# A two-layer decoder trunk: first vectors loaded from ScalarE's queue, and three early steps traced ahead of the state-space parameters

## The chip, the core and the metric

The kernel is one program on one NeuronCore of a Trainium2 chip. The core has five instruction streams that concern us: TensorE (PE in the profile, with its weight loads as PEld), VectorE (DVE), ScalarE (ACT), GpSimd (POOL) and SyncE (SP). Each stream runs its instructions in order and waits on semaphores for the others. Transfers between HBM and on-chip memory are issued by SP, ACT or POOL as one instruction each and are then carried out by the 16 DMA engines. The metric is device time in microseconds (us); lower is better.

## What is computed

The reference is two layers of a causal decoder over 512 tokens of width 1024, in float32. Only the start of layer 0 matters here:

```python
hn = rms_norm(x, norm_mix_pre[0])        # norm factor per token, gain g0 per column
z = hn @ ev_w_in                         # 1024 -> 512 q, 512 k, 512 v, 512 u
q, k, v = ...                            # rotary, then dilated attention
a_bar = exp(A * dt); b_bar = (a_bar - 1) / A * B     # S5 state-space parameters
h = scan(a_bar, einsum(b_bar, u)); y = Re(C h) + D u # S5 layer on u
x = x + rms_norm([att, glu(gelu(y))] @ ev_w_out, norm_mix_post[0])
```

Behind it come a SwiGLU feed-forward block, a second layer with a gated recurrence, and a second feed-forward block.

## The kernel before

**Matrix products.** Every product of float32 operands is split: an operand is rounded to a short-mantissa float32 (`hi`, an ACT copy at L240 for weights) and the remainder is kept (`lo`, a DVE subtraction at L241). Three matmuls, hi·hi, hi·lo and lo·hi, make one float32 product (L170 is the line of all of them). A weight chunk of two 128-row blocks is loaded by SP (L216, 256 KB for each block), split, used, and its places are given back; 22 places of 128x512 go round.

**The start of layer 0.** The program is traced in this order. `s5_first` (L308 to L316) issues six small loads from ACT's queue: the step size `s5dt`, four loads of the state-space rows `s5rows`, and a piece of the constants `cst`. `load_vecs(0, ...)` (L298) issues four loads of 8 KB from POOL's queue: the gains g0, p0, g1, p1, one row of 128 values for each partition. SP then loads x (`xtok`, eight pieces of 256 KB, L294) alternating with the u weights (`wraw_u`, eight of 256 KB), and after that the C matrix of the state-space layer and the rest. A second set of vectors goes through POOL. `turn_vecs` (L360) transposes g0 on PE so that it lies along partitions (`cols`).

`even_layer` (L1151) then works on halves h of the tokens and pairs of columns f. PE transposes x into a bank (`xps`), ACT scales it by g0 and rounds it (`xh`, L541), DVE takes the remainder (`xl`, L542), and PE accumulates u, without the norm factor, in four PSUM banks (`ub`, banks 0 to 3). The norm factor is a scalar per token and is multiplied in when u is evacuated.

After this loop `s5_params` (L910) is traced: some 80 small operations on tiles of 128x32 to 128x288, most on DVE, in long chains of dependent steps. It makes the tables' inputs `a1`, `a2`, `m1`, `m2` and the phases `ka`, `kb`. Then the norm factor (L1183 to L1196): eight squares of x with a sum on ACT (`xsq`, L1189), a power on POOL, a broadcast by PE into bank 6 (`bc_m`), and an ACT copy to on-chip memory (`bcs_m`, L405). Then u is evacuated: four DVE multiplications (`up`, L1200) of the `ub` banks by the factor, each followed by a store to a scratch buffer in HBM (`ud`, L1203), which the state-space pieces read back reordered (`s5u`).

**What follows.** `even_body` (L1212) computes q, k and v (`qkv_gemm`), each 8 blocks of weights times four token tiles t, in four banks. The banks of q are 4, 0, 1, 2, so that token tile 0 uses a free bank and tiles 1 to 3 use banks that `ub` held. Eight pieces of the state-space layer (`s5_piece`) are traced between the matmuls of q, k and v by a clock that the program counts by hand. A piece begins with a table `em` from `m1`, `m2` (L1027 to L1029) that PE transposes (`s5eps`).

**Order.** The program is traced as a list. The context is opened with `schedule_with_timeline_sim=True`, so a scheduler makes each stream's order from that list at build time: work that is ready may go ahead of work that was traced earlier, and among ready work the earlier traced goes first. From k on (`pe_order`) PE keeps the program's order.

Of the kernel before, what the change touches and what calls it, by code (L numbers as in the profile page):

```python
# [19 lines left out]
P = 128  # L20
# [74 lines left out]
def hybrid_trunk(  # L95
# [8 lines left out]
    nc = tc.nc  # L104
    dve, act, pool = nc.vector, nc.scalar, nc.gpsimd
# [4 lines left out]
    def dump(name, ap):  # L110
        if dbg is not None and name in dbg:
            nc.sync.dma_start(dbg[name], ap)
# [8 lines left out]
    def bank(name, use="main"):  # L121
        q = sets[use]
        q.append(q.pop(0))
        return psum.tile([P, 512], F32, tag=f"bank{q[-1]}", name=name)

    def side(name):
        return bank(name, "side")
# [128 lines left out]
    def wchunk(src, nk, n, nm, **kw):  # L256
        return Chunk(Raw(nk, n, nm, src), nm, **kw)
# [5 lines left out]
    def wrows(w, k0, nk, c0, nm, **kw):  # L263

        return wchunk(w[k0 * P:(k0 + nk) * P, c0:c0 + 512].rearrange("(k p) n -> p k n", p=P), nk, 512, nm, **kw)
# [20 lines left out]
    tabp = tab_cm.__enter__()  # L286
# [3 lines left out]
    vecs = [fp.tile([SP, P], F32, name=f"vec{i}") for i in range(2)]  # L290
# [4 lines left out]

    vcol = {}

    def load_vecs(i, lst):  # L298
        row = 0
        for nm, ap in lst:  # L300
            f = ap.flatten_outer_dims() if len(ap.shape) > 2 else ap
            n = int(np.prod(ap.shape)) // P
            pool.dma_start(vecs[i][row:row + n, :], f.rearrange("a (b c) -> (a b) c", c=P))
            vcol[nm] = i * SP + row
            row += n
        assert row == SP

    def s5_first():  # L308

        rows = fp.tile([SG, 4, SP], F32, name="s5rows")  # L310
        dt = fp.tile([P, SG], F32, name="s5dt0")
        nc.scalar.dma_start(dt, s5_log_dt.partition_broadcast(P))
        for i in range(2):
            nc.scalar.dma_start(rows[:, i, :], s5_a_re[0])
            nc.scalar.dma_start(rows[:, 2 + i, :], s5_a_im[0])
        nc.scalar.dma_start(cst[:, C_JR:], consts[:, C_JR:])  # L316
        s5_raw.update(rows=rows, dt=dt)
# [8 lines left out]
        s5_raw.update(drow=drow, cc=cc)  # L326

    s5_raw = {}
    s5_first()
    load_vecs(0, (("g0", norm_mix_pre), ("p0", norm_mix_post), ("g1", norm_ffn_pre), ("p1", norm_ffn_post)))  # L330
    uw = []
    for h in range(2):
        load_x(0, h)
# [76 lines left out]
    def xg_tiles(nm):  # L410
        return ([sb.tile([P, S], F32R, tag="xh", bufs=NF, name=f"xh_{nm}{f}") for f in range(NF)],
                [sb.tile([P, S], F32R, tag="xl", bufs=NF, name=f"xl_{nm}{f}") for f in range(NF)])
# [127 lines left out]
    def x_split(src, h, l, g):  # L540
        act.activation(h, src, AF.Copy, scale=g)  # L541
        return dve.scalar_tensor_tensor(l, src, g, h.bitcast(F32), op0=ALU.mult, op1=ALU.subtract)  # L542
# [608 lines left out]
    def even_layer():  # L1151
        w = ev_w_in[0]
        xh, xl = xg_tiles("m0")

        ub = [bank(f"ub{i}") for i in range(4)]
        x_first = []
        s5_turn_a()
        for h in range(2):
            for f0 in range(0, NF, 2):
                b = side(f"xps{h}{f0}")  # L1160
                for i in range(2):
                    for t in range(2):
                        o = i * HT + t * P
                        pe.transpose(b[:, o:o + P], xtok[2 * h + t][:, (f0 + i) * P:(f0 + i + 1) * P], ident)
                for i in range(2):
                    src = b[:, i * HT:(i + 1) * HT]
                    split = x_split(src, xh[f0 + i][:, HS[h]], xl[f0 + i][:, HS[h]], col("g0", f0 + i))
                    act.activation(xT[f0 + i][:, HS[h]], src, AF.Copy)
                if f0 == XSQ:
                    x_first.append(split.ins)  # L1170
                w2 = uw[f0 // 2]
                for k in (f0, f0 + 1):
                    for i in range(4):
                        mm3(ub[i][:, HS[h]], [a[:, i * P:(i + 1) * P] for a in w2(k % 2)], xh[k][:, HS[h]],
                            xl[k][:, HS[h]], k == 0, k == NF - 1)
                if h == 1:
                    w2.free()
            if h == 0:
                T = s5_turn(tabp)
                turn_vecs(0, NF)  # L1180
                turn_vecs(1)
        s5_params(tabp, T)
        ssum = sb.tile([P, NT], F32, name="ssum0")  # L1183
        sx = sb.tile([P, NT], F32, name="sx0")
        for t in range(NT):
            for h, s in enumerate((ssum, sx)):
                j = sb.tile([P, S], F32, tag="sq", bufs=2, name=f"xsq{t}{h}")
                with tc.issue_after(x_first[t // 2]):
                    act.activation(j, xtok[t][:, h * 512:(h + 1) * 512], AF.Square, accum_out=s[:, t:t + 1])  # L1189
        dve.tensor_tensor(ssum, ssum, sx, op=ALU.add)  # L1190
        r1 = rstd_of(ssum, NT, "m0")
        rq = sb.tile([P, NT], F32, name="rq")
        dve.tensor_scalar(rq, r1, -0.125, None, op0=ALU.mult)
        r = sb.tile([P, NT], F32, name="r0")
        dve.tensor_copy(r, r1)
        rb = bcast_sb(r, "m0")  # L1196
        uds = []
        for q in range(4):
            up = sb.tile([P, TC, NK], F32, tag="gt" if q < 2 else "ut", bufs=2, name=f"up{q}")
            dve.tensor_tensor(up.rearrange("p i k -> p k i")[:, :, ::-1], ub[q].rearrange("p (k i) -> p k i", i=TC),  # L1200
                              rb.rearrange("p (k i) -> p k i", i=TC), op=ALU.mult)
            ud = dr.tile([P, S], F32, name=f"ud{q}")
            nc.sync.dma_start(ud, up.rearrange("p i k -> p (i k)"))  # L1203
            uds.append(ud)
            dump(f"u{q}", up.rearrange("p i k -> p (i k)"))
        first_cm.__exit__(None, None, None)
        with tc.tile_pool(name="even", bufs=1) as lp:
            got = even_body(w, xh, xl, r, rq, uds, T, lp)
        tab_cm.__exit__(None, None, None)
        return got  # L1210

    def even_body(w, xh, xl, r, rq, uds, T, lp):  # L1212
        share(qkv=(4, 0, 1, 2, 3), s5z=(5,), s5w=(6,), s5y=(7,), turn=(2,))

        posf = sb.tile([P, HT], F32, tag="sqh", bufs=2, name="posf")[0:NT, 0:P]
# [1 line left out]
        b = bank("posps", "s5w")  # L1217
# [26 lines left out]
        def qkv_gemm(s, at_k=lambda k: None):  # L1244
            banks = [bank(f"qkv{s}{t}", "qkv") for t in range(NT)]
            for k0 in range(0, NF, 2):
                w2 = wrows(w, k0, 2, s * 512, f"qkv{s}{k0}")
                for kk in range(2):
                    k = k0 + kk
                    hi, lo = w2(kk)  # L1250
                    for t in range(NT):
                        tt = slice(t * P, t * P + P)
                        pe.matmul(banks[t], lhsT=xh[k][:, tt], rhs=hi, start=(k == 0), stop=False)
                        pe.matmul(banks[t], lhsT=xh[k][:, tt], rhs=lo, start=False, stop=False)
                        pe.matmul(banks[t], lhsT=xl[k][:, tt], rhs=hi, start=False, stop=(k == NF - 1))
                        tick()
                    at_k(k)
                w2.free()
            ts = []
            for t in range(NT):  # L1260
                of = lp.tile([P, S], F32, tag="av", bufs=4, name=f"v{t}") if s == 2 else spare(t, f"qk{s}{t}")
                o = of.rearrange("p (h d) -> p h d", d=HD)
                act.activation(of, banks[t], AF.Copy, scale=(rq if s == 0 else r)[:, t:t + 1])
                ts.append(o)
                if s < 2:

                    cb = rcs[:, t].unsqueeze(1).to_broadcast([P, HEADS, 2, RH])
                    sbb = rsn[:, t].unsqueeze(1).to_broadcast([P, HEADS, 2, RH])
                    tv = o[:, :, 0:2 * RH].rearrange("p h (a f) -> p h a f", a=2)
                    tm = lp.tile([P, HEADS, 2, RH], F32, tag="rp0", bufs=2, name=f"rp{s}{t}")  # L1270
                    dve.tensor_tensor(tm, tv[:, :, ::-1], sbb, op=ALU.mult)
                    dve.tensor_tensor(tv, tv, cb, op=ALU.mult)
                    dve.tensor_tensor(tv, tv, tm, op=ALU.add)
            return ts
# [344 lines left out]
    xh, xl, first, nsum = even_layer()  # L1619
    for f in range(NF):  # L1620
        dump(f"x1_{f}", xT[f])
    xh, xl, first, nsum = ffn(0, xh, xl, first, nsum)
# [4 lines left out]
    xh, xl, first, nsum = odd_layer(xh, xl, first, nsum)  # L1627
# [34 lines left out]
```

## Time and profile before

| what | value |
|---|---|
| time, three runs | 1175.7, 1176.76, 1180.08 us; median 1176.76 |
| the profiled execution | 1172.18 us, of which the profile's span is 1170.2 us |
| granted TensorE clock, mean | 0.995 of full |
| busy, share of the span | PE 97%, PEld 86%, DVE 75%, ACT 54%, POOL 5% |
| moved | 113.45 MB, 97 GB/s on average |

The span runs from the first to the last instruction; the 2 us around it are not in the profile. A row of the timeline gives the start, the duration, the engine, the line of the program, the operation, what it writes and reads, and in brackets how long the engine sat idle before it and what ended that. `x3` behind a row means that three like instructions are merged. ACTq and SPq are the queues of transfers on those streams: their rows are issues, not the movement of data.

### The profile page before, as it was taken

The numbers are of one execution on the slowest core, as the hardware profiler recorded it, in microseconds if no ns is written. First come the engines' busy times: TensorE is split into PE (matmuls) and PEld (weight loads), VectorE is DVE, ScalarE is ACT, GpSimd is POOL, SyncE is SP. The second block draws the span as 40 slices with busy tenths as digits, with TensorE's granted clock in tenths as the row PEclk, the third lists the DMA queues.
The fourth block names the chain that finished last, engine by engine and source line by source line (L and its number), as shares of the span: only waits on it lengthen the run. The fifth ranks groups of instructions, "written<-read, shape, count | busy, mean of one in ns | idle before, by whom it ended". The sixth has DMA issues, their size and how long they took to land.

```text
span 1170.2 us, 20253 instructions
## 1 busy us (share of the span) xinstructions
PE 1129.9 (97%) x7550; PEld 1010.3 (86%) x7550; DVE 878.1 (75%) x1841; ACT 629.2 (54%) x1290; POOL 60.5 (5%) x101
## 2 busy tenths in 40 slices
PE   6899999999999999999999999999999999999997
PEld 6777766789899999988889987889999999988886
DVE  7978875567999899983445896966999899994224
ACT  7556567446754545662243469744955455582221
POOL 2000010004000000000002200004000000000001
PEclk9899999999999999999999999999999999999999
DMA  8254420431343323332340333340253343234221
GB/s 214 97 147 123 104 73 1 141 95 28 110 119 97 91 85 106 94 121 92 114 121 1 91 91 90 121 132 1 73 144 95 91 118 95 85 123 123 93 63 72
DMA packets 165273, 113.45 MB, mean 97 GB/s; under 512 B 26820, under 2 KB 141752, under 8 KB 165176
## 3 DMA queue, kind: packets, MB, share of 16 engines
q1 hardware_dynamic: 161848, 109.94, 32.2%
q10 hardware_dynamic: 3040, 2.17, 0.7%
q8 instruction: 59, 0.97, 0.4%
q14 instruction: 38, 0.31, 0.1%
q0 software_dynamic: 288, 0.07, 0.0%
HBM read 103.75 MB, written 4.19 MB: 92 GB/s over the span
## 4 chain that ended last, share of the span: by engine, by line
PE 78%; ACT 8%; DMA 6%; DVE 5%; issue 2%; POOL 1%; SPq 0%; ACTq 0%; DVEq 0%; POOLq 0%
PE fo L170 10%; PE op_fd L170 10%; PE qkv L170 5%; PE f00b L170 5%; PE f02b L170 5%; PE f01b L170 4%; PE f11b L170 4%; PE op_mo L170 4%; PE f12b L170 4%; PE f10b L170 4%; PE gg L170 3%; PE f03b L170 2%; PE f13b L170 2%; PE xbb L170 2%; PE fd0b L170 2%
## 5 line engine op out<-in xcount | busy, mean ns | idle before, releaser
L241 DVE TENSOR_TENSOR wlo_fo<-wraw_fo,whi_fo 128x512 fp32r<-128x512 f32 x44 | 30.2, 691 | 63.6 <-PE fo L170 55.4
L170 PE MATMUL op_fd<-hi_f,whi_fd 128*128 128x512 f32 (+1 forms) x200 | 73.6, 368 | 0.0
L170 PE MATMUL op_fd<-lo_f,whi_fd 128*128 128x512 f32 (+1 forms) x200 | 73.3, 366 | 0.0
L170 PE MATMUL op_fd<-hi_f,wlo_fd 128*128 128x512 f32 (+1 forms) x200 | 72.9, 368 | 0.0
L170 PE MATMUL fo<-wlo_fo,hi_f 128*128 128x512 f32 x176 | 69.6, 395 | 0.0
L170 PE MATMUL fo<-whi_fo,lo_f 128*128 128x512 f32 x176 | 69.2, 394 | 0.0
L170 PE MATMUL fo<-whi_fo,hi_f 128*128 128x512 f32 x176 | 68.9, 396 | 0.0
L240 ACT ACTIVATE whi_fo<-wraw_fo 128x512 fp32r<-128x512 f32 x44 | 27.6, 631 | 70.2 <-DMA wraw_fo<-in_ffn_w_down_dram 43.8
L241 DVE TENSOR_TENSOR wlo_fd<-wraw_fd,whi_fd 128x512 fp32r<-128x512 f32 x44 | 30.0, 690 | 46.5 <-ACT whi_fd L240 40.4
L240 ACT ACTIVATE whi_fd<-wraw_fd 128x512 fp32r<-128x512 f32 x44 | 27.4, 629 | 55.0 <-DMA wraw_fd<-in_ffn_w_down_dram 34.2
L170 PEld LDWEIGHTS op_fd<-lo_f,whi_fd 128*128 128x128 f32 x200 | 37.7, 189 | 6.9
L170 PE MATMUL qkv<-whi_qkv,xh_m 128*128 128x512 f32 x96 | 42.1, 440 | 1.5 <-DVE up L1200 1.3
L170 PEld LDWEIGHTS op_fd<-hi_f,wlo_fd 128*128 128x128 f32 x200 | 37.7, 188 | 6.7
L170 PEld LDWEIGHTS op_fd<-hi_f,whi_fd 128*128 128x128 f32 x200 | 37.7, 188 | 6.5
L170 PE MATMUL qkv<-wlo_qkv,xh_m 128*128 128x512 f32 x96 | 39.2, 408 | 2.6 <-DVE wlo_qkv L241 2.6
L170 PEld LDWEIGHTS fo<-whi_fo,lo_f 128*128 128x128 f32 x176 | 33.1, 188 | 7.8
L170 PEld LDWEIGHTS fo<-whi_fo,hi_f 128*128 128x128 f32 x176 | 33.1, 188 | 7.7
L170 PEld LDWEIGHTS fo<-wlo_fo,hi_f 128*128 128x128 f32 x176 | 33.1, 188 | 7.5
L170 PE MATMUL qkv<-whi_qkv,xl_m 128*128 128x512 f32 x96 | 39.0, 407 | 0.0
L638 DVE TENSOR_TENSOR wraw_s_f<-wraw_f,wraw_f 128x512 f32<-128x512 f32 x40 | 27.3, 683 | 10.6 <-DMA wraw_f<-in_ffn_w_up_dram 7.5
L241 DVE TENSOR_TENSOR wlo_mo<-wraw_mo,whi_mo 128x512 fp32r<-128x512 f32 x32 | 21.4, 685 | 15.3 <-ACT whi_mo L240 15.1
L639 DVE TENSOR_TENSOR wraw_t_f<-wraw_s_f,wraw_f 128x512 f32<-128x512 f32 x40 | 27.2, 681 | 5.6 <-DMA wraw_f<-in_ffn_w_gate_dram 5.6
(1975 smaller groups left out, 4289.2 us busy)
## 6 DMA issues: line engine op xcount, KB each, us to landing
wraw_f<-in_ffn_w_gate_dram SPq DMA_DIRECT2D x88, 256.0 KB, 3.2
wraw_f<-in_ffn_w_up_dram SPq DMA_DIRECT2D x88, 256.0 KB, 3.4
wraw_fd<-in_ffn_w_down_dram SPq DMA_DIRECT2D x44, 256.0 KB, 2.7
wraw_fo<-in_ffn_w_down_dram SPq DMA_DIRECT2D x44, 256.0 KB, 2.9
wraw_qkv<-in_ev_w_in_dram SPq DMA_DIRECT2D x24, 256.0 KB, 3.5
wraw_mo<-in_ev_w_out_dram SPq DMA_DIRECT2D x16, 256.0 KB, 5.2
wraw_xb<-in_od_w_in_dram SPq DMA_DIRECT2D x16, 256.0 KB, 2.9
wraw_gg<-in_od_w_in_dram SPq DMA_DIRECT2D x16, 256.0 KB, 2.9
```

What stands on the lines that cost most here:

```text
L170: self.pin(nc.tensor.matmul(o, lhsT=lhsT, rhs=rhs, start=start, stop=stop, **kw))
L240: act.activation(hi, src, AF.Copy)
L241: eng.tensor_tensor(lo, src, hi.bitcast(F32), op=ALU.subtract)
L638: dve.tensor_tensor(s1, a21, a22, op=ALU.add)
L639: dve.tensor_tensor(s2, s1, a11, op=ALU.subtract)
```

## The change

Three things move; no arithmetic changes.

1. The four loads of g0, p0, g1, p1 are issued by ACT instead of POOL, and ahead of the six small loads that ACT issues already.
2. The weights of the first two chunks of q (k0 = 0 and 2) are traced directly after the loop over u, ahead of the norm factor, and handed to `qkv_gemm`.
3. `s5_params` is traced after the norm factor and the evacuation of u, no longer ahead of them.

```diff
-    def load_vecs(i, lst):
+    def load_vecs(i, lst, q=pool):
...
-            pool.dma_start(vecs[i][row:row + n, :], f.rearrange("a (b c) -> (a b) c", c=P))
+            q.dma_start(vecs[i][row:row + n, :], f.rearrange("a (b c) -> (a b) c", c=P))
...
     s5_raw = {}
+    load_vecs(0, (("g0", norm_mix_pre), ("p0", norm_mix_post), ("g1", norm_ffn_pre), ("p1", norm_ffn_post)),
+              nc.scalar)
     s5_first()
-    load_vecs(0, (("g0", norm_mix_pre), ("p0", norm_mix_post), ("g1", norm_ffn_pre), ("p1", norm_ffn_post)))
...
-        s5_params(tabp, T)
+        qw = {k0: wrows(w, k0, 2, 0, f"qkv0{k0}") for k0 in (0, 2)}
         ssum = sb.tile([P, NT], F32, name="ssum0")
...
             dump(f"u{q}", up.rearrange("p i k -> p (i k)"))
+        s5_params(tabp, T)
         first_cm.__exit__(None, None, None)
...
-                w2 = wrows(w, k0, 2, s * 512, f"qkv{s}{k0}")
+                w2 = (qw.pop(k0, None) if s == 0 else None) or wrows(w, k0, 2, s * 512, f"qkv{s}{k0}")
```

More of the change, by code (lines that the diff above doesn't have):

```diff
@@ L1205, in even_layer, with even_body @@
             dump(f"u{q}", up.rearrange("p i k -> p (i k)"))
+        s5_params(tabp, T)
         first_cm.__exit__(None, None, None)
         with tc.tile_pool(name="even", bufs=1) as lp:
-            got = even_body(w, xh, xl, r, rq, uds, T, lp)
+            got = even_body(w, xh, xl, r, rq, uds, T, lp, qw)
         tab_cm.__exit__(None, None, None)
         return got
-    def even_body(w, xh, xl, r, rq, uds, T, lp):
+    def even_body(w, xh, xl, r, rq, uds, T, lp, qw):
         share(qkv=(4, 0, 1, 2, 3), s5z=(5,), s5w=(6,), s5y=(7,), turn=(2,))
```

## Prediction

> **What bounds the kernel now.** I read the page first, then the waits of PE, then the timeline of the first 60 us, since everything that moves lies there. The page says PE: busy nearly all of the span, and most of the chain that ended last.
>
> ```profile
> PE 1129.9 (97%) x7550; PEld 1010.3 (86%) x7550; DVE 878.1 (75%) x1841; ACT 629.2 (54%) x1290; POOL 60.5 (5%) x101
> ...
> PE 78%; ACT 8%; DMA 6%; DVE 5%; issue 2%; POOL 1%; SPq 0%; ACTq 0%; DVEq 0%; POOLq 0%
> ```
>
> So 40 us of 1170 are not PE at work. The waits of PE in the first 150 us show those that the change could touch: the first vector, then a pair near 50 us.
>
> ```profile
> PE vps L181 <- DMA vec<-in_norm_mix_pre_dram: 5.3, 1, 5.3
> PE qkv L170 <- DVE wlo_qkv L241: 2.6, 1, 2.6
> ...
> PE qkv L170 <- DVE up L1200: 1.3, 1, 1.3
> ```
>
> The pair costs more than its waits. The busy time by stretch (stretch, length, then PE, PEld, DVE, ACT and POOL with their counts, granted clock, DMA share, GB/s) shows 25 us in which PE is nearly full, then 5.1 us with PE at 1.3, then 5.8 us at a granted clock of 0.50:
>
> ```profile
> 20.00:45.00 25.00, 24.17 (x187) 22.86 (x188) 22.82 (x80) 17.91 (x47) 1.49 (x2) 1.00 0.42 86
> ...
> 48.00:53.10 5.10, 1.31 (x5) 0.62 (x4) 5.10 (x11) 2.62 (x7) 0.10 (x1) 0.91 0.01 2
> 53.10:58.90 5.80, 5.78 (x14) 4.52 (x15) 5.80 (x11) 0.00 (x0) 0.00 (x0) 0.50 0.72 231
> ```
>
> DVE is full in both. The evacuation of u is what PE waits for there: q's token tiles 1 to 3 need the banks that `ub` holds. Its factor is ready when ACT's `bcs_m` ends at 48.07, yet DVE does other work first:
>
> ```profile
> 46.95 0.63 ACT L240 ACTIVATE whi_qkv<-wraw_qkv 128x512 fp32r<-128x512 f32 x1 [1.40 <-DMA wraw_qkv<-in_ev_w_in_dram]
> ...
> 47.49 0.58 ACT L405 ACTIVATE bcs_m<-bc_m 128x512 f32<-128x512 f32 x1
> ```
>
> ```profile
> 48.55 0.68 DVE L1027 TENSOR_TENSOR s5em<-s5b,s5m 128x512 f32<-128x512 f32 x1
> ...
> 51.37 0.75 DVE L1044 TENSOR_TENSOR s5gm<-s5cT,s5a 128x576 f32<-128x576 f32 x1
> 52.05 1.02 DVE L1200 TENSOR_TENSOR up<-ub,bcs_m 128x512 f32<-128x512 f32 x1
> ...
> 52.92 2.86 DVE L1200 TENSOR_TENSOR up<-ub,bcs_m 128x512 f32<-128x512 f32 x3
> ...
> 55.68 0.68 DVE L1029 TENSOR_TENSOR s5em<-s5em,s5tn 128x512 f32<-128x512 f32 x1
> ```
>
> What stands ahead of `up` is not `s5_params`, which the change moves; its last copy on ACT is over at 45.6:
>
> ```profile
> 45.13 0.42 ACT L1008 ACTIVATE s5m<-s5mi 64x256 f32<-64x256 f32 x1
> ```
>
> It is the tables, L1027 and L1044, traced *behind* `up` already. They went first because the scheduler held them ready sooner. So tracing `s5_params` later does not by itself bring `up` forward; it does so only if the tables, which need the results of `s5_params`, become ready later than `up`.
>
> **The change part by part.** *The four loads on ACT* come first in time. Here are ACT's first instructions, then SP's:
>
> ```profile
> 0.73 0.41 ACTq L312 DMA_DIRECT2D s5dt<-in_s_log_dt_dram  x1
> 1.18 0.44 ACTq L314 DMA_DIRECT2D s5rows<-in_s_a_re_dram  x1
> 1.65 0.44 ACTq L315 DMA_DIRECT2D s5rows<-in_s_a_im_dram  x1
> 2.12 0.44 ACTq L314 DMA_DIRECT2D s5rows<-in_s_a_re_dram  x1
> 3.76 0.32 ACTq L315 DMA_DIRECT2D s5rows<-in_s_a_im_dram  x1
> 4.85 0.35 ACTq L316 DMA_DIRECT2D cst<-in_consts_dram  x1
> 5.23 1.28 ACT L240 ACT_TABLE_LOAD   x1 [5.23 <-DMA s5rows<-in_s_a_re_dram]
> ```
>
> ```profile
> 0.73 0.39 SPq L284 DMA_DIRECT2D cst<-in_consts_dram  x1
> 1.18 0.89 SPq L294 DMA_DIRECT2D xtok<-in_x_dram  x2
> 2.11 0.43 SPq L216 DMA_DIRECT2D wraw_u<-in_ev_w_in_dram  x1
> ```
>
> Each issue takes 0.44 us, and then there are gaps: the fifth issue of ACT comes at 3.76, the sixth at 4.85. SP's queue shows what such a gap is. A weight load there waits for a load that has nothing to do with it:
>
> ```profile
> SPq L216 <- DMA s5dt<-in_s_log_dt_dram: 1.4, 1, 1.4
> ```
>
> Taking both queues in order of issue, s5dt, cst, x, s5rows, x, s5rows, u, s5rows fill eight places, and the ninth transfer waits for the first to land, the tenth for the second. I read it as eight completion slots that SP and ACT use in turn; POOL's loads, which went out every 0.5 us without a gap, are not among them. The change puts four more loads into this rotation, at its head. The times from issue to landing in the first 30 us (last number, median):
>
> ```profile
> xtok<-in_x_dram SPq DMA_DIRECT2D x8, 256.0 KB, 5.4
> ...
> s5rows<-in_s_a_im_dram ACTq DMA_DIRECT2D x2, 8.0 KB, 3.7
> ...
> s5dt<-in_s_log_dt_dram ACTq DMA_DIRECT2D x1, 16.0 KB, 3.2
> vec<-in_norm_mix_pre_dram POOLq DMA_DIRECT2D x1, 8.0 KB, 4.0
> ```
>
> If both queues go on issuing in turn, ACT's ten loads are g0, p0, g1, p1, s5dt, four s5rows, cst. The last has the slot of the first s5rows, which has the slot of p0. p0 goes out at 1.18 and lands 3.7 later at 4.88; s5rows then lands at 8.58; cst is issued, 0.35, and ACT is free at 8.93 where it was at 5.20: 3.73 later. Behind it on ACT stand the table load, the split of the first u weights and the first xh, for which PE waits. Of the delay, the idle time that ACT has there now is absorbed:
>
> ```profile
> 7.89 0.63 ACT L240 ACTIVATE whi_u<-wraw_u 128x512 fp32r<-128x512 f32 x1 [0.61 <-DMA wraw_u<-in_ev_w_in_dram]
> 8.42 0.46 ACT L541 ACTIVATE xh_m<-xps,cols 128x256 fp32r<-128x256 f32 x1
> ...
> 9.66 0.63 ACT L240 ACTIVATE whi_u<-wraw_u 128x512 fp32r<-128x512 f32 x1 [0.17 <-DMA wraw_u<-in_ev_w_in_dram]
> ```
>
> ```profile
> 8.93 1.23 PE L170 MATMUL ub<-xh_m,whi_u 128*128 128x256 f32 x4 [1.09 <-ACT xh_m L541]
> ```
>
> That is 3.73 - 0.61 - 0.17 = 2.95 us. From there to 45 us PE is full (24.17 of 25), so nothing takes it back; later x and u loads slip by 1 to 3 us by the same rotation, no more than their users. The fourth s5rows, which PE's next transposes need, takes the slot of s5dt: 3.76 + 3.2 = 7.0, landing at 10.7, before the xh that PE waits for anyhow (8.42 + 2.95 + 0.46 = 11.8). The gain on the other side is nothing: g0 comes perhaps 0.3 us sooner (3.7 against 4.0), but what PE does after `vps` needs x, and then xh from ACT. Bounds: +0.98 if no slot ever binds (four issues of 0.44 less 0.78), +5 or more if the loads land slowly. I take 2.95.
>
> The Trainium skill, "DMA: Bandwidth & Descriptors", section "Issuing engines are not separate DMA queues", says that issuing from more engines saves only the sequencer's time of issue, usually small beside the transfer. By that rule alone the move would cost ACT its issues and no more, which is the lower bound; the wait of a weight load for s5dt in this trace speaks for the higher.
>
> *The q weights and the norm factor, 0.* The first chunk is split already while `s5_params` runs, and PE can use it for token tile 0 alone until `up` has run. The factor `r` is there at 25.4, and its broadcast runs at 44.00, when the u loop leaves PE and bank 6 to it:
>
> ```profile
> 24.50 0.67 DVE L241 TENSOR_TENSOR wlo_qkv<-wraw_qkv,whi_qkv 128x512 fp32r<-128x512 f32 x1
> ...
> 25.27 0.15 DVE L1195 COPY r<-rsy_m 128x4 f32<-128x4 f32 x1
> ...
> 44.00 0.38 PE L170 MATMUL bc_m<-cst,r 128*128 128x128 f32 x2
> ```
>
> *`s5_params` later.* Its price, if its tables came late, has cover: the first `em` is complete at 56.4, PE transposes it first at 67.3.
>
> ```profile
> L181 PE MATMUL s5eps<-cst,s5em x16: 270/272/273, 67.3 to 97.1; 128*128 128x128 f32 x16
> ```
>
> So it costs nothing unless it slips by over 10 us. What it may bring is `up` ahead of the tables. If `up` ran right behind `bcs_m`, it would start at 48.07 instead of 52.05: 4.0 us. Fourteen matmuls would also run at full clock: twelve take 2.84 there, so fourteen 3.3 instead of 5.8, 2.5 us. Together 6.5.
>
> ```profile
> 103.12 2.84 PE qkv L170 x12
> ```
>
> The Trainium skill's page "TensorE: Matmul & The Clock Gate", on the two states of the clock, has half rate end after some 3.4 us of work. The trace has half rate for 5.8 us behind this gap, so it does not agree. By the page half of 3.4, or 1.7 us, would come back, and the sum would be 5.7.
>
> I take 0 for the middle as the likeliest. `s5_params` loses its place only to a few small or already early steps, and its first inputs come later by about as much as xh, so that tables and `up` most likely meet in the old order. So the sum is +2.95 + 0 = +2.95. The profiled execution took 1172.18 and would take 1175.1. The median of the runs is 1176.76, 4.6 above that execution; the difference goes onto the median: **1179.7**.
>
> **The rivals.** *The middle opens as well.* The tables become ready after `up`, DVE evacuates first, 6.5 us come back less 2.95: 1173.2. For it: only `bcs_m` and a handful of DVE operations separate the two orders. Against: nothing that `up` needs is brought forward.
>
> *No slot binds, issue time only:* 1176.76 + 0.98 = 1177.7. Against it stands s5dt's row.
>
> *The front costs much more (slower).* ACT's last issue stands behind two landings in a row. Landings of 5.4 us, as x has them, instead of 3.7 give 1.18 + 5.4 + 5.4 + 0.35 = 12.33, 7.13 later than 5.20, less 0.78: +6.35, or 1183.1. It decides from landings of about 5.2 on. For it: ten small and six big transfers now share the first microseconds. Against: the small ones landed in 3.2 to 3.9.
>
> *The front costs nothing and the middle opens:* 1176.76 - 6.5 = 1170.3. It needs ACT's loads to be put behind its first splits.
>
> **How the numbers follow.** Forecast 0.40, middle opens 0.25, issue time only 0.12, costly front 0.13, only gain 0.10. A measurement of this kernel tells about 0.5%, 5.9 us, from no change: faster is below 1170.9, slower above 1182.6. The only-gain case lies just past the first: 0.08, and 0.05 from the middle's case where the front costs less. The costly front lies at the other edge: 0.10, and 0.04 from the forecast's upper tail. The rest, 0.73, is no change. The range takes the only-gain case at one end and the costly front at the other, 1170 to 1183.5; between lie the forecast and the two rivals near it, whose signs differ, and the forecast's own range is 1177.7 to 1182.
>
> **What would show it.** Right: ten loads on ACT with gaps among the last six; the table load near 8.9; the first xh near 11.4; the first `ub` matmul near 11.9 instead of 8.93; the end of u some 3 us later; L1027 and L1044 still ahead of `up`; a stretch of half clock behind it. Wrong: a table load before 7.5 breaks the first step; `up` directly behind `bcs_m`, with no half clock in q, breaks the second; either moves the time to the case that names it. A wait of PE for `s5em` would show that the late `s5_params` has no cover.

## The result, and the profile after

The changed kernel takes 1191.49 us (median of 1184.43, 1190.95, 1192.03 and 1193.25), the kernel before 1177.49 in the same measurement (median of four, 1175.7 to 1180.08): a ratio of 1.0108 over the runs (1.0119 for the two medians), with a 95% interval of 1.0075 to 1.0141. It is slower by 1.1%, and lies outside the predicted range of 1170 to 1183.5. The profiled execution took 1184.43 us (span 1182.6) against 1172.18 (span 1170.2), so the two traces carry 12.25 of the 14 us.

TensorE (PE) still bounds the kernel. It is busy 6.4 us longer for the same 7550 matmuls, and its share of the chain fell:

```profile
PE 1136.3 (96%) x7550; PEld 1015.4 (86%) x7550; DVE 876.9 (74%) x1841; ACT 628.6 (53%) x1290; POOL 58.4 (5%) x97
...
PE 75%; DVE 8%; DMA 7%; ACT 6%; issue 2%; POOL 1%; ACTq 0%; SPq 0%; DVEq 0%; POOLq 0%
```

ScalarE's (ACT's) first instructions in the timeline (start, duration): ten issues with gaps from the fifth on, and the table load at 8.94, where the prediction had read 8.93 off the rotation of eight slots. Behind it come four weight splits ahead of the first xh, where before had two.

```profile
2.12 0.44 ACTq L303 DMA_DIRECT2D vec<-in_norm_ffn_post_dram  x1
2.76 0.36 ACTq L312 DMA_DIRECT2D s5dt<-in_s_log_dt_dram  x1
3.99 0.37 ACTq L314 DMA_DIRECT2D s5rows<-in_s_a_re_dram  x1
4.62 0.32 ACTq L315 DMA_DIRECT2D s5rows<-in_s_a_im_dram  x1
6.97 0.32 ACTq L314 DMA_DIRECT2D s5rows<-in_s_a_re_dram  x1
7.97 0.32 ACTq L315 DMA_DIRECT2D s5rows<-in_s_a_im_dram  x1
8.56 0.35 ACTq L316 DMA_DIRECT2D cst<-in_consts_dram  x1
8.94 1.28 ACT L240 ACT_TABLE_LOAD   x1 [8.94 <-DMA s5rows<-in_s_a_im_dram]
10.23 2.19 ACT L240 ACTIVATE whi_u<-wraw_u 128x512 fp32r<-128x512 f32 x4
12.33 0.45 ACT L542 ACTIVATE xh_m<-xps,cols 128x256 fp32r<-128x256 f32 x1
```

On PE the gains are used 2.45 us sooner (2.87 instead of 5.32), and nothing comes of it, since the first product of u waits for xh and starts at 12.84 instead of 8.93:

```profile
2.87 0.24 PE L181 MATMUL vps<-cst,vec 8*128 8x8 f32 x1 [2.87 <-DMA cst<-in_consts_dram]
...
12.84 1.22 PE L170 MATMUL ub<-xh_m,whi_u 128*128 128x256 f32 x4 [2.10 <-ACT xh_m L542]
16.37 0.58 PE L170 MATMUL ub<-xl_m,whi_u 128*128 128x256 f32 x1 [2.31 <-DVE xl_m L543]
```

On VectorE (DVE) the tables still stand ahead of `up`, and now also ahead of the last xl of u, which in the kernel before began at 41.33:

```profile
51.08 0.68 DVE L1028 TENSOR_TENSOR s5em<-s5b,s5m 128x512 f32<-128x512 f32 x1
...
51.68 0.48 DVE L543 SCALAR_TENSOR_TENSOR xl_m<-xps,cols,xh_m 128x256 fp32r<-128x256 f32 x1
52.08 0.75 DVE L1045 TENSOR_TENSOR s5gm<-s5cT,s5a 128x576 f32<-128x576 f32 x1
...
55.97 1.03 DVE L1201 TENSOR_TENSOR up<-ub,bcs_m 128x512 f32<-128x512 f32 x1
```

The account is made best by three stages: up to the first product of u, from there to `up`, and from `up` to the first product of the attention (`asc`). These are the busy times by stretch (stretch, length, then PE, PEld, DVE, ACT and POOL with their counts, granted clock, DMA share, GB/s), before and then after:

```profile
0.00:8.93 8.93, 2.52 (x11) 2.03 (x11) 3.58 (x26) 2.96 (x5) 4.89 (x13) 1.00 0.69 190
8.93:52.05 43.12, 37.70 (x265) 33.90 (x265) 39.85 (x128) 32.95 (x82) 1.91 (x5) 1.00 0.55 143
52.05:151.78 99.73, 94.50 (x543) 76.30 (x543) 80.83 (x192) 52.94 (x113) 1.72 (x12) 0.95 0.47 130
```

```profile
0.00:12.84 12.84, 3.07 (x12) 1.97 (x12) 4.20 (x29) 3.89 (x7) 2.95 (x9) 1.00 0.70 221
12.84:55.97 43.13, 38.17 (x264) 34.64 (x265) 40.68 (x129) 31.95 (x80) 1.59 (x5) 1.00 0.51 129
55.97:162.47 106.50, 98.53 (x545) 79.91 (x544) 78.52 (x187) 52.34 (x113) 1.79 (x12) 0.90 0.42 117
```

The first stage is 3.91 us longer. The second has the same length to 0.01 us, so that `up` is as late as the first product; the experiments show how far that is chance. The third, in which no step that the change moved is left, is 6.77 us longer. In it PE stands idle for 7.97 us instead of 5.23, and works 4.0 us longer on the same matmuls at a granted clock of 0.90 instead of 0.95. Behind the attention come another 1.7 us, and that makes the 12.4 of the span. The 1.7 fit one stretch of 3.41 us at half clock, at 256.0, that the kernel before doesn't have (half of 3.41 is 1.7). So two things have to be explained: 3.9 us of front, and 6.8 us in a stage that the change doesn't touch.

### The profile page after: what moved, and what is told of

Its sections match the earlier page's. It is cut to its first block, busy times and chain, and to the rows that moved or that the text cites. A ratio compares the mean times of both kernels' runs of the same rounds, so it can differ in the third digit from the quotient of the medians.

```text
span 1182.6 us, 20244 instructions
## 1 busy us (share of the span) xinstructions
PE 1136.3 (96%) x7550; PEld 1015.4 (86%) x7550; DVE 876.9 (74%) x1841; ACT 628.6 (53%) x1290; POOL 58.4 (5%) x97
## 4 chain that ended last, share of the span: by engine, by line
PE 75%; DVE 8%; DMA 7%; ACT 6%; issue 2%; POOL 1%; ACTq 0%; SPq 0%; DVEq 0%; POOLq 0%
PE fo L170 10%; PE op_fd L170 10%; PE f02b L170 5%; PE f00b L170 5%; PE f01b L170 4%; PE op_mo L170 4%; PE f11b L170 4%; PE f10b L170 4%; PE f12b L170 4%; PE qkv L170 3%; PE gg L170 3%; PE f03b L170 2%; PE f13b L170 2%; PE xbb L170 2%; PE mo1b L170 2%
## 6 DMA issues: line engine op xcount, KB each, us to landing
wraw_f<-in_ffn_w_gate_dram SPq DMA_DIRECT2D x88, 256.0 KB, 3.1
wraw_f<-in_ffn_w_up_dram SPq DMA_DIRECT2D x88, 256.0 KB, 3.3
wraw_fd<-in_ffn_w_down_dram SPq DMA_DIRECT2D x44, 256.0 KB, 2.7
wraw_fo<-in_ffn_w_down_dram SPq DMA_DIRECT2D x44, 256.0 KB, 2.9
wraw_qkv<-in_ev_w_in_dram SPq DMA_DIRECT2D x24, 256.0 KB, 3.6
wraw_mo<-in_ev_w_out_dram SPq DMA_DIRECT2D x16, 256.0 KB, 4.5
wraw_xb<-in_od_w_in_dram SPq DMA_DIRECT2D x16, 256.0 KB, 3.0
wraw_gg<-in_od_w_in_dram SPq DMA_DIRECT2D x16, 256.0 KB, 2.9
```

## The experiments

Each is compared with the kernel before in the same measurement. The first-product, `up` and attention times are from the one profiled execution of each; the last column but one is the length of the third stage. Executions of one kernel differ too (26 of the kernel before took 1170.5 to 1185.1 us), so a difference of a microsecond or two between two stages says little. "VectorE's order" compares the list of VectorE's steps (operation and tiles) between `up` and the attention with that of the kernel before: the longest series of steps that both have in the same order, as a share of the steps of both.

| run | ratio, interval | first u product | `up` | attention | third stage | VectorE's order |
|---|---|---|---|---|---|---|
| before | 1 | 8.93 | 52.05 | 151.78 | 99.7 | 1 |
| changed | 1.0108, 1.0075 to 1.0141 | 12.84 | 55.97 | 162.47 | 106.5 | 0.69 |
| e1_act_only | 1.0093, 1.0057 to 1.0129 | 12.88 | 56.77 | 167.32 | 110.5 | 0.69 |
| e2_order_only | 1.0001, 0.9973 to 1.0028 | 9.24 | 54.37 | 152.99 | 98.6 | 0.99 |
| e4_act_behind | 1.0138, 1.0095 to 1.0182 | 12.5 | 60.07 | 171.32 | 111.3 | 0.62 |
| e5_g0_act | 1.0071, 1.0044 to 1.0098 | 10.5 | 54.42 | 158.57 | 104.2 | 0.71 |
| e7_all_pool | 0.9971, 0.9946 to 0.9995 | 7.33 | 46.39 | 150.87 | 104.5 | 0.58 |
| e9_swap | 1.0019, 0.9996 to 1.0041 | 10.3 | 47.65 | 154.62 | 107.0 | 0.60 |
| e10_after_fill | 1.0103, 1.0065 to 1.0140 | 15.3 | 58.20 | 165.67 | 107.5 | 0.73 |
| e11_after_xsq | 1.0078, 1.0051 to 1.0105 | 12.3 | 56.06 | 161.55 | 105.5 | 0.79 |
| e13_fill3 | 1.0078, 1.0050 to 1.0106 | 13.2 | 56.51 | 162.31 | 105.8 | 0.73 |
| e12_before_xsq | 1.0031, 1.0008 to 1.0053 | 9.07 | 51.82 | 156.99 | 105.2 | 0.78 |
| e14_pool_xsq | 1.0048, 1.0021 to 1.0076 | 8.0 | 47.23 | 153.54 | 106.3 | 0.57 |
| e8_pool_order | 1.0010, 0.9990 to 1.0031 | 8.5 | 46.61 | 154.10 | 107.5 | 0.58 |
| e15_pad | 1.0155, 1.0125 to 1.0185 | 11.01 | 63.30 | 169.65 | 106.3 | 0.69 |
| e16_split_order | 1.0092, 1.0062 to 1.0121 | 11.61 | 56.06 | 164.43 | 108.4 | 0.76 |
| e17_sp | 1.0078, 1.0052 to 1.0104 | 10.61 | 53.10 | 159.84 | 106.7 | 0.74 |
| e18_after_lo | 1.0141, 1.0109 to 1.0173 | 12.8 | 60.34 | 168.42 | 108.1 | 0.68 |
| e19_before_lo | 1.0156, 1.0112 to 1.0200 | 9.46 | 57.00 | 164.57 | 107.6 | 0.65 |
| e20_pool_lo | 1.0067, 1.0038 to 1.0097 | 8.5 | 49.35 | 162.94 | 113.6 | 0.66 |

### Which part of the change it is

**e1_act_only** makes the first part alone: `load_vecs` ahead of `s5_first`, on `nc.scalar`.

> Only the four loads move to the head of ACT's queue; the program's order of the three steps is that of before. Theory F (the front carries the loss): ACT's table load again near 8.9 us, the first u matmul near 12.8 instead of 8.9, the second xh near 18, u done near 53 instead of 45; the time 8 to 15 us above before. Rival M (the moved steps carry the loss, with s5_params late): u done at most 4 us later than before, the time within 4 us of before.

**e2_order_only** makes the second and third part alone; the gains stay on GpSimd.

> Only the order changes: first q weights, norm factor and evacuation of u ahead of s5_params; the four loads stay on POOL. Theory F: first u matmul at 8.9 and u done near 45 as before; the time within 4 us of before, with the middle (45 to 60 us) deciding the sign. Rival M: 8 to 15 us above before, with waits of PE for s5 tables or for the turned q between 80 and 150 us.

**e4_act_behind** issues the gains from ACT behind the six loads of the state-space layer, and **e5_g0_act** moves g0 alone:

```diff
-            pool.dma_start(vecs[i][row:row + n, :], ...)
+            (nc.scalar if nm == "g0" else pool).dma_start(vecs[i][row:row + n, :], ...)
...
-    s5_first()
     load_vecs(0, (("g0", norm_mix_pre), ...))
+    s5_first()
```

> The four loads go to ACT's queue but behind the six that it has. Theory F in its first form (ACT is held by the count of its issues, each waiting for the landing eight back in the common order of SP and ACT): still ten issues, so the table load near 8.9 again, the first xh near 12, and the time 8 to 15 us above before. Rival R (what costs is that s5dt and s5rows come late): these come as in before, so the loss goes and the time is within 4 us of before.

> Only g0 goes to the head of ACT's queue, p0, g1 and p1 stay on POOL: seven issues on ACT instead of six. Theory F: the last issue waits for a landing near 5.5, ACT is free near 5.9 instead of 5.2, which its idle time of 0.8 us absorbs: first u matmul 8.7 to 9.5, time within 3 us of before. If each small load ahead of the s5 loads costs a share of the loss by itself: about 3 us above before.

The first part is the whole loss (1.0093 against 1.0108, intervals overlapping), and the other two are nothing that could be measured (1.0001). The order of the ten loads doesn't help: behind the six they cost as much or more (1.0138, intervals overlapping). One load moved costs over half of what four do, though ACT's table load comes only 1.47 us later (6.70); "within 3 us" was missed. The loss doesn't grow in step with the delay. In e4 s5dt is used at 3.94, as in the kernel before (3.95), so what is lost there is not lost by late state-space inputs; its gains come late instead.

Nor is the delay of the first product simply handed on to `up`. The second stage takes 43.9 us in e1 and 45.1 in e2 against 43.1 before, and 37.3 to 52.3 over the whole table. That it came out equal in the changed kernel is in part chance.

### Is it ACT, or the transfers?

**e7_all_pool** takes all ten small loads off ACT, the gains first on GpSimd's queue. **e9_swap** is the changed kernel with only the six state-space loads on GpSimd; the gains stay on ACT.

```diff
-        nc.scalar.dma_start(dt, s5_log_dt.partition_broadcast(P))
+        pool.dma_start(dt, s5_log_dt.partition_broadcast(P))
...
-            nc.scalar.dma_start(rows[:, i, :], s5_a_re[0])
+            pool.dma_start(rows[:, i, :], s5_a_re[0])
...
```

> The other direction: ACT issues no early load at all, the ten small loads all go out from POOL (the gains first), the rest as before. Theory F (issues on ACT hold its first splits, and small loads take places in the rotation of SP): table load before 2 us, first u matmul before 8.9, SP's x and u loads earlier than before, u done before 45, the time 2 to 8 us below before. Rival R (late state-space rows cost): POOL's ten issues of 0.5 us put s5rows at about 8 to 10 us, and the time is above before.

> The kernel after with the six state-space loads on POOL: ACT issues only the four gains, in 1.8 us, none of which has to wait for a landing. Theory F: table load near 2.6 us, first u matmul at or before 8.9, u done by 46, so the loss of the kernel after goes (time within 4 us of before or below). If the four gain loads cost by themselves: 8 us or more above before.

With four small loads on ACT instead of ten the loss is gone (1.0019), although the first product is still 1.4 us late (10.3, "at or before 8.9" was missed), as PE waits up to 2.7 us for a piece of x. With none on ACT the kernel is slightly faster than before (0.9971): the best version of this study. In e7 ACT's table load stands at 0.72, and `up` runs right behind `bcs_m`, as one rival of the prediction had it:

```profile
0.72 1.28 ACT L1189 ACT_TABLE_LOAD   x1 [0.72 <-PEq L1648]
...
45.22 0.58 ACT L405 ACTIVATE bcs_m<-bc_m 128x512 f32<-128x512 f32 x1
```

```profile
46.39 1.04 DVE L1200 TENSOR_TENSOR up<-ub,bcs_m 128x512 f32<-128x512 f32 x1
...
55.03 0.68 DVE L1027 TENSOR_TENSOR s5em<-s5b,s5m 128x512 f32<-128x512 f32 x1
```

`up` is 5.66 us ahead of the kernel before, but the attention only 0.91: the third stage gives back 4.75. Part of that is work that has only moved: the tables that stood ahead of `up` now stand behind it, and VectorE is busy there for 88.0 us instead of 80.8. The same holds for the other four kernels with all small loads on GpSimd or only the gains on ACT (e8, e9, e14, e20: 85.6 to 88.8).

**e15_pad** holds ACT without touching a load: the kernel before with an idle copy behind its six issues. The fill of its tile also holds VectorE from 1.54 to 4.58.

```diff
-        nc.scalar.dma_start(cst[:, C_JR:], consts[:, C_JR:])
+        last = nc.scalar.dma_start(cst[:, C_JR:], consts[:, C_JR:])
+        pad = fp.tile([P, 3584], F32, name="pad")
+        dve.memset(pad, 1.0)
+        with tc.issue_after(last.ins):
+            act.activation(pad, pad, AF.Copy)
```

> The kernel before with one idle copy of 128x3584 on ScalarE behind its six loads, some 3.8 us; its result is used nowhere. The loads keep their queues and their order. If ScalarE's late start by itself makes the loss: first xh at 11 to 12 us, u done at 50 to 54, attention's first product at 157 to 165 where before has 151.8, ratio 1.006 to 1.011. If the later loads of x and u through the shared slots make what goes beyond the late start: everything is some 3 to 4 us late and no more, attention at 155 to 156, ratio 1.002 to 1.004.

**e17_sp** does the opposite: the gains at the head of SP's queue (`load_vecs(..., nc.sync)` ahead of `s5_first`), so that the loads of x and u are late and ACT is not held.

> The kernel before with the four gain loads at the head of SyncE's queue, behind its first 64 KB constants, no longer on GpSimd's. x and u loads start four issues, 1.8 us, later and take their slots behind the small ones; ScalarE issues its own six loads alone, and its table load comes at 5 to 6.5 us. If the loss needs ScalarE to be held: ratio 0.999 to 1.004, u done by 48. If late loads of x and u are what costs: ratio 1.006 to 1.011, u done at 50 to 54 although the table load is early.

Either costs about what the change costs, 1.0155 and 1.0078; neither theory was right as stated. In e15 the first product is only 2.1 us late, and the wait of PE for xl inside the u loop adds the most: `up` is 11.25 late. In e17 the fourth gain load waits for its slot until 4.13 although its three forerunners went out every 0.46 us, which shows the rotation of eight again on SP's side (it is the tenth issue of the two queues, and s5dt, the second, is used by VectorE from 4.14 on); the first product is 1.7 us late, `up` 1.05, the attention 8.06:

```profile
1.17 0.42 SPq L303 DMA_DIRECT2D vec<-in_norm_mix_pre_dram  x1
1.64 0.41 SPq L303 DMA_DIRECT2D vec<-in_norm_mix_post_dram  x1
2.09 0.42 SPq L303 DMA_DIRECT2D vec<-in_norm_ffn_pre_dram  x1
4.13 0.31 SPq L303 DMA_DIRECT2D vec<-in_norm_ffn_post_dram  x1
```

```profile
53.10:159.84 106.74, 95.31 (x545) 76.78 (x545) 80.02 (x189) 52.65 (x113) 1.72 (x12) 0.94 0.44 121
```

So once more the larger part arises behind `up`, in the third stage.

### Is it TensorE's cold clock?

In the changed kernel PE works at half pace until 23.9 us (14.7 before). **e10_after_fill** and **e13_fill3** put idle matmuls into its early waits (the diff is that of e13; e10 has 8 in place of the 3, and not the second part):

```diff
-        s5_turn_a()
+        s5_turn_a(); wb = bank("warm", "turned"); [... nc.tensor.matmul(wb[:, 0:P], lhsT=ones, rhs=ones, ...) for _ in range(3)]
...
+                    if h == 0 and k == 0:
+                        for _ in range(10):
+                            nc.tensor.matmul(wb[:, 2 * P:4 * P], lhsT=w2(0)[0][:, 0:P], rhs=xh[0][:, HS[0]], ...)
```

> The kernel after with 8 extra matmuls on constant data on PE, in the wait between the second s5pps transpose (10.7 us) and the first u matmul (12.8). They compute nothing that is used. Theory C (a part of the loss is TensorE at half rate until 23.9 us, against 14.7 before): full rate from 14 to 18 us on, u done 1 to 3 us sooner than in the kernel after, with the first u matmul and the xh where they were. Rival A (the u loop is held by ACT's and DVE's splits, the half rate costs nothing): u done within 0.5 us of the kernel after.

> The changed kernel with 13 idle matmuls more on TensorE: 3 of 128x128 in float32 behind the first transposes, and 10 of 128x256 behind the first four matmuls of u, where TensorE waits 2.3 us for the first remainder xl. Their results are used nowhere. Theory clock (part of the loss is that TensorE stays at half rate until 23.9 us): with the wait filled the first full-clock record comes between 15 and 21 us, the u loop ends 1 to 3 us before 53.4, and the time is about 1188 where the changed kernel has 1191.5. Rival (the splits on ScalarE and VectorE pace the u loop): full clock comes sooner as well, but u ends at 53 to 54 and the time stays at 1190 to 1192.

e10 settles nothing: its fillers took 3.8 us and delayed the first product to 15.3. In e13 the fillers lie in the wait for xl, and full pace comes at 17.0. The u loop ends 1.1 us sooner, at 52.4, as the theory had it, but `up` and the attention stay where they were (56.51 and 162.31 against 55.97 and 162.47).

```profile
14.20 2.33 PE L1179 MATMUL warm<-xh_m,whi_u 128*128 128x256 f32 x10
...
17.25 0.28 PE L170 MATMUL ub<-xh_m,wlo_u 128*128 128x256 f32 x1
```

So the cold front sets neither of the two. The time, 1.0078, is lower than the changed kernel's, but lies within its interval: a gain of some 3 us is neither shown nor excluded.

### Is it the order that the scheduler makes?

**e16_split_order** keeps the loads of the change, and traces the later weight splits behind the x split of the step before, so that ACT again does two weight splits and then xh.

```diff
-        uw += [wrows(ev_w_in[0], k0, 2, 1536, f"u{k0}") for k0 in (4 * h, 4 * h + 2)]
+        for k0 in (4 * h, 4 * h + 2):
+            raw = Raw(2, 512, f"u{k0}", ...)
+            uw.append(raw if k0 else Chunk(raw, "u0"))
...
+                if h == 0 and f0 + 2 < NF:
+                    uw[f0 // 2 + 1] = Chunk(uw[f0 // 2 + 1], f"u{f0 + 2}")
```

> The changed kernel with the splits of the second and later u weights traced behind the x split of the step before, so that ScalarE does two weight splits, xh, and then the next two, as in the kernel before. If the order that the scheduler chose is a cause: first xh at 11.3 us where the changed kernel has 12.33, u done 1 to 3 us sooner than 53.4, ratio 1.006 to 1.009. If not: xh 1 us sooner, u done and the time as in the changed kernel, ratio 1.009 to 1.012.

**e11_after_xsq** and **e12_before_xsq** issue the squares of the norm factor on ACT only behind the fourth xh (`x_split` returns ACT's instruction, on which the squares then wait), in the changed kernel and in the one before; **e14_pool_xsq** does so in e7.

```diff
-                if f0 == XSQ:
+                if f0 == XSQ + 2:
```

> The kernel after with the squares of the norm factor issued on ACT behind the fourth xh of their half. Theory A (ACT's order between the first and the second xh, with squares in it, is what holds PE from 13 to 18 us): second xh near 16.5 instead of 18.1, u done 1.5 to 3 us sooner, the time 2 to 5 us below the kernel after. Theory C alone (only the rate of TensorE): no change in the time beyond 1 us unless full rate comes sooner too.

> The kernel before with one edit: the squares of x for the norm factor are traced and issued on ScalarE behind the fourth xh, no longer behind the second. If ScalarE's early order costs time whatever starts ScalarE late, the second xh comes sooner than 12.5 us, u ends 1 to 2 us before 45.3 and the time falls by 1 to 4 us (ratio 0.997 to 0.999). If the order costs only where ScalarE starts late, no difference: ratio 0.999 to 1.001.

> The kernel before with all ten small loads on GpSimd's queue, gains first, and the squares behind the fourth xh. The loads alone gave 0.9971. If the two gains add up: table load near 0.7, u done near 41 to 42.9, ratio 0.993 to 0.997. If ScalarE, once it starts at 0.7, has room for the squares anyway: the same as the loads alone, 0.996 to 0.998.

**e8_pool_order** adds the second and third part of the change to e7.

> All ten small loads on GpSimd's queue, gains first, with the second and third parts of the change (first q weights and norm factor and evacuation of u traced ahead of the state-space parameters). If these two parts cost and bring nothing where ScalarE starts early either: ratio 0.996 to 0.998, as the loads alone, and the tables still ahead of the evacuation. If they let the evacuation run first once the front is early: no half clock near 50 us, and a ratio of 0.991 to 0.994.

e16 puts the first product at 11.61, 2.68 us late instead of 3.91, so the other 1.2 us of the front are the scheduler's order on ACT. The u loop ends 2.1 us sooner, yet `up` is where it was (56.06), the attention comes 2 us later, and the time is as in the changed kernel. In e11 the u loop ends 3.0 us sooner, but `up` and the attention are within 1 us of the changed kernel's; its time, 1.0078, again lies within the changed kernel's interval.

```profile
10.05 1.15 ACT L240 ACTIVATE whi_u<-wraw_u 128x512 fp32r<-128x512 f32 x2
11.10 0.46 ACT L544 ACTIVATE xh_m<-xps,cols 128x256 fp32r<-128x256 f32 x1
```

e12 is the run that tells most. Its first product is 0.14 us behind the kernel before. The u loop ends 3.0 us later (48.3 against 45.3), but `up` comes 0.23 us ahead all the same. Yet its third stage takes 5.44 us more, with PE just as long busy (94.35 against 94.50) and idle for 10.8 us instead of 5.2:

```profile
9.07:51.82 42.75, 37.28 (x262) 33.58 (x262) 39.38 (x129) 33.35 (x82) 1.75 (x5) 1.00 0.56 143
51.82:156.99 105.17, 94.35 (x545) 76.66 (x546) 81.40 (x193) 52.58 (x113) 1.72 (x12) 0.95 0.44 123
```

The trace shows where most of that idle time arises. PE turns q and k, four tiles at a time, into one bank (`tr`), and ACT copies the bank out (`qkT`); PE can't turn the next four before that. In the kernel before, the sixth of these copies stands on ACT ahead of a step of the state-space layer (`s5cs`), in e12 behind it, and that step waits for VectorE, which waits for a transfer (`s5xg`, 2.46 us). So the copy comes 6.9 us behind its transposes instead of 2.2, and PE waits 6.12 us instead of 0.90. The longest wait of the changed kernel is of the same kind: its copy comes 4.7 us behind its transposes. Before, e12 and changed:

```profile
135.95 0.66 PE L181 MATMUL tr<-cst,qk 128*128 128x128 f32 x4 [0.90 <-ACT qkT L1284]
135.31 0.59 ACT L1284 ACTIVATE qkT<-tr 128x512 f32<-128x512 f32 x1
136.12 0.51 ACT L1058 ACTIVATE s5cs<-s5sn,magic 128x256 f32<-128x256 f32 x1 [0.22 <-DVE s5sn L1056]
```

```profile
139.19 1.12 PE L181 MATMUL tr<-cst,qk 128*128 128x128 f32 x4 [6.12 <-ACT qkT L1285]
137.56 0.51 ACT L1059 ACTIVATE s5cs<-s5sn,magic 128x256 f32<-128x256 f32 x1 [1.97 <-DVE s5sn L1057]
138.55 0.59 ACT L1285 ACTIVATE qkT<-tr 128x512 f32<-128x512 f32 x1
```

```profile
144.88 1.12 PE L181 MATMUL tr<-cst,qk 128*128 128x128 f32 x4 [2.75 <-ACT qkT L1286]
142.58 0.42 ACT L1063 ACTIVATE s5cs<-s5sn 128x256 f32<-128x256 f32 x1 [2.16 <-DVE s5sn L1062]
144.25 0.57 ACT L1286 ACTIVATE qkT<-tr 128x512 f32<-128x512 f32 x1
```

e2 is the counterpart of e12: `up` 2.32 us late, VectorE's order nearly that of the kernel before (0.99), and a third stage of 98.6.

```profile
54.37:152.99 98.62, 93.34 (x545) 75.14 (x543) 80.90 (x192) 52.59 (x113) 1.73 (x12) 0.96 0.45 126
```

In e8 the second and third part seem to take e7's small gain away again (1.0010, intervals touching): `up` is 0.2 us later, the third stage 3.0 us longer.

In all the table the third stage takes 98.6 or 99.7 us where VectorE's order is kept, and 104.2 to 113.6 in the eighteen where it isn't, whether `up` comes early (46.4) or late (63.3). So its length goes with whether the order is kept, and not with the time at which it begins. Among the eighteen it doesn't go with the share that is kept, and in five of them VectorE also has more to do there. The expectations for e12 and e14 (a gain, or nothing) were missed: moving eight squares on ACT was enough to have 100 us behind them put in another order.

### Is VectorE the bound of the start?

VectorE is busy for 39.85 of the 43.12 us of the second stage. **e18_after_lo**, **e19_before_lo** and **e20_pool_lo** compute four of the eight u remainders on GpSimd, in the changed kernel, in the one before and in e7:

```diff
-        uw += [wrows(ev_w_in[0], k0, 2, 1536, f"u{k0}") for ...]
+        uw += [wrows(ev_w_in[0], k0, 2, 1536, f"u{k0}", eng=pool if k0 >= 4 else dve) for ...]
```

> The changed kernel with four of the eight remainders of the u weights (0.67 us each on VectorE, L241) computed by GpSimd, which is nearly idle there. Theory (VectorE's backlog is the bound from 10 to 70 us): the evacuation of u starts 2 to 3 us before 55.97, attention at 157 to 160 where the changed kernel has 162.5, ratio 1.004 to 1.009. Rival (VectorE is not the bound): evacuation and attention where they were, ratio 1.009 to 1.012. If GpSimd is so slow that TensorE waits for it: u done after 54, ratio over 1.012.

> The kernel before with the same four remainders on GpSimd. Theory: evacuation of u 2 to 3 us before 52.05, ratio 0.996 to 0.999. Rival: ratio 0.999 to 1.002. GpSimd too slow: over 1.002.

> All ten small loads on GpSimd's queue, gains first (0.9971 by itself), with the same four remainders on GpSimd. Theory: the two add, ratio 0.992 to 0.996. Rival: 0.996 to 0.998. GpSimd too slow: over 0.999.

e19 and e20 were slower than the kernels they start from; e18, with 1.0141, can't be told from the changed kernel. PE did not only wait for GpSimd's results: GpSimd held VectorE up. In e19 GpSimd's four subtractions run for 5.56 us, and in that time VectorE gets through four steps, which take 0.45, 0.18, 0.45 and 0.17 us in the kernel before:

```profile
14.71 5.56 POOL L241 TENSOR_TENSOR wlo_u<-wraw_u,whi_u 128x512 fp32r<-128x512 f32 x4 [8.43 <-ACT whi_u L240]
```

```profile
14.92 1.54 DVE L863 SCALAR_TENSOR_TENSOR s5la<-ex_k_mag,s5la 128x288 f32<-128x288 f32 x1
16.38 1.27 DVE L836 SCALAR_TENSOR_TENSOR s5th<-wr_th,s5th 128x32 f32<-128x32 f32 x1
17.58 1.58 DVE L864 SCALAR_TENSOR_TENSOR s5la<-ex_k_mag,s5la 128x288 f32<-128x288 f32 x1
19.08 1.23 DVE L842 TENSOR_SCALAR s5th<-s5th 128x32 f32<-128x32 f32 x1
```

The edit took more from VectorE (5.6 us for 1.2 us of work, some 4.4 us) than it gave (four times 0.68), so the question is only half answered. What it does show: with the first product only 0.5 us late and VectorE held between 15 and 20 us, `up` is 4.95 us late. The Trainium skill, "SBUF — State Buffer", section "SBUF: two separate sides", says that GpSimd and VectorE (in a two-port mode, or with two operands in that memory) share a pair of ports, which one instruction holds for its whole length; the four rows agree with that.

## Why the prediction was wrong

**The four loads on ACT: right in mechanism.** The rotation gave 8.93 for ACT's table load, measured 8.94. The chain is the one that was named: s5rows goes out when p0 has landed (3.99), and cst when that s5rows has (8.56). That the sum fits to 0.01 us is luck. Both landings were put at 3.7 us, but p0 took 2.8 and s5rows 4.6. The Trainium skill's "DMA: Bandwidth & Descriptors", section "Issuing engines are not separate DMA queues", would have had only the issue time as the difference; the gaps in ACT's ten issues don't agree. In e9 the gains cost ACT their four issues alone (table load at 2.59), and there the loss is gone.

**"That is 3.73 - 0.61 - 0.17 = 2.95 us": mis-sized.** The first product was 3.91 late. e16 gives the reason: with two weight splits ahead of xh it is 2.68, close to the 2.95. The prediction took ACT's order of before for granted, and the scheduler had made another one, with four splits.

**"From there to 45 us PE is full, so nothing takes it back": right to `up` in the number, not shown in the reason.** From the first product to `up` both kernels take 43.12 and 43.13 us, but over the runs this stage takes 37.3 to 52.3, so the equality is in part luck. PE being full is not shown to be what hands the delay on: filling PE's waits (e13) left `up` where it was, and with VectorE held (e19) it was late.

**"So the sum is +2.95 + 0": the step that failed.** The 0 stands for the second and third part, and for these by themselves it is right in the time, as e2 shows; L1027 and L1044 did stay ahead of `up`. But the prediction weighed only whether `up` comes ahead of the tables. The sum has no term for the stretch from `up` to the attention: it was put at nothing without a reason, and what the first part does to the order of those 100 us was not asked. That stage measured +6.8 us, 2.7 of it in waits of PE and 4.0 in longer work, with 20.5 us at half clock instead of 10.2; 1.7 more came behind the attention. The waits of the stage for qkT and the state-space pieces (total, times, longest), before and then after:

```profile
PE tr L181 <- ACT qkT L1284: 2.5, 2, 1.6
...
PE s5w L170 <- ACT s5bw L1093: 0.6, 2, 0.5
```

```profile
PE tr L181 <- ACT qkT L1286: 4.7, 3, 2.7
...
PE s5w L170 <- ACT s5bw L1094: 2.5, 2, 1.5
```

The predicted half clock behind `up` is not there (`up` to 75 us runs at 1.00). Instead there are 6.8 us of it from 95.6 on and 13.7 near the end of the stage (136.6 to 150.2; what the prediction read as 5.8 us in the kernel before is 6.83 in the trace's own record of the clock):

```profile
136.00:151.00 15.00, 12.25 (x51) 10.05 (x54) 10.08 (x24) 9.18 (x20) 0.30 (x2) 0.54 0.29 71
```

**The rivals.** The costly front (1183.1) has the nearest time, but by slow landings that would put ACT's table load at 12.33; it came at 8.94. Some small loads were slow all the same (s5dt was issued at 2.76 and used by VectorE as it landed, at 7.97); that this cost anything behind the front isn't shown. That the middle opens happened in e7, and brought 0.91 us at the attention rather than 6.5: the order behind it changed too, and the tables' work moved behind `up`.

**Still open.** No run has the loads on ACT together with the order of before in the third stage. That the order makes the third stage long rests on e2 and e12, on the waits for qkT and on the table, not on a run that puts the order back. How much of the 4.0 us of longer work at half clock belongs to the order, and how much to that one execution, is not shown. The waits for qkT explain e12 and a part of the changed kernel, not every long third stage (in e18 they are 2.0 us); and why e15's u loop is so long was not isolated.

## What to carry to other kernels

Where a scheduler makes the order of the engines' streams at build time, an edit at the head changes the work far behind it: compare the two orders before pricing the edit, look for a copy that an in-order engine now does behind a step that waits, and price the stretch that is reordered, not only the stretch that is edited. An issue of a transfer is not free on an engine that computes: ten small loads on ACT held its first computation for 8.9 us, and moving them to an idle engine's queue gave the only version that was faster than both kernels (0.9971). Judge a gain at a place where all engines meet again (here the attention), since 5.7 us won at `up` were 0.9 there.

## What the runs showed of the hardware

- In these kernels SP and ACT share eight places for transfers under way: the ninth and the tenth issue of the two queues wait for the landings of the first two. In the kernel before the ninth goes out at 3.76; in e17 the tenth goes out at 4.13, as s5dt lands; in the changed kernel ACT's sixth waits until 3.99 for p0.
- Half-clock stretches came in multiples of 3.41 us (6.83 and 13.65 in the third stage of the changed kernel), although no wait of PE there is longer than 2.75 us, and the last waits ahead of the two stretches are 1.3 and 0.9 us. The Trainium skill, "TensorE: Matmul & The Clock Gate", section "HAM oscillation — how this bites in real kernels", gives as its rule that PE should have no idle gaps of over about 3.4 us; shorter ones were enough here, so the trace does not agree.
- The granted clock of the stretches reads 1.00 from the start, yet PE's matmuls of 128x256 follow each other every 0.21 us until 23.9 us and every 0.12 behind. The first record of full clock in a trace (23.9 here, 14.7 in the kernel before), not the column, tells where the cold start ends.
- One GpSimd subtraction of 128x512 took 1.4 us, and while four of them ran VectorE finished one step for each.
